# Plain float32 products for compressed keys, values and queries, compressed biases on TensorE, and a later layer norm, in a hybrid decoder block

## The chip, the core and the metric

The kernel runs on one core of one Trainium2 chip. The metric is the device time of one execution in microseconds (us). The engines of the core run side by side, each with its own in-order queue: PE (TensorE, matrix products; PEld is its loading of weights), DVE (VectorE), ACT (ScalarE), POOL (GpSimd) and SP, which here only issues transfers.

## The reference

One decoder layer for 256 positions and 1024 features, float32 throughout. Cut to what matters here:

```python
h = rms_norm(x, norm_mix_g)
u_conv, q, kc, vc, ks, vs, kw, vw, g_heads, g_conv, g_attn = split(h @ w_in)
# conv: gated, causal depthwise with 31 taps over 1024 channels, layer norm, silu, pointwise
v = a * sigmoid(gt); v = depthwise31(v) + dw_b
conv_out = silu(layer_norm(v, ln_g, ln_b)) @ pw_w
# compressed branch: 15 blocks of 32 keys, stride 16
k_cmp = silu((kc_blocks + pos) @ w1) @ w2          # the same for v_cmp
s_c = q @ k_cmp * scale + rel_bias[bucket(t - c_end)]
o_cmp = masked_softmax(s_c, t - c_end >= 0) @ v_cmp
# selected and window branches: for 256 positions both see every causal key,
# each with its own keys and values, both with rel_bias[bucket(t - k)]
o = g0 * o_cmp + g1 * o_slc + g2 * o_win
x = x + (sigmoid(g_conv) * conv_out + sigmoid(g_attn) * o) @ w_out
x = x + cross_attention(rms_norm(x), mem)
x = x + swiglu(rms_norm(x)); out = rms_norm(x)
```

There are 16 heads of 64 features in 4 key groups; kc, vc, ks, vs, kw and vw have 256 columns each, q has 1024. The bias depends only on the distance, through 32 buckets.

## The kernel before

Features lie on the 128 partitions, positions in the free dimension. The weights are streamed in chunks of 1024 x 256 (named k0 to k3, u0 to u7, kc, vc, q0 to q3, ks, kw, vs, vw, ga0 to ga3 and so on); a chunk comes in two halves of 512 KB, each a transfer on SP into one of three load tiles (tag "w", L138 and L139).

*Split products.* Almost every product is made from three matmuls in the format fp32r. `split` (L126) parts a half chunk into a rounded part `hi` (a copy on ACT, L129) and a rest `lo` (a subtraction, L131, on DVE; for a few early halves on POOL). The activations are parted in the same way (`hh`, `hl` for h). `product` (L146) then multiplies hi by hi, hi by lo and lo by hi. `gemm` (L151) does so for a whole chunk: 2 blocks of columns x 8 blocks of features x 3 = 48 matmuls into one PSUM bank, taken in turn from two (`bank`, L97, tag "mm"). The tags "s", "s0", "pt" and "o" hold six more banks for scores, transposes, the convolution's sums and outputs.

*The order.* The text of the kernel is the order in which instructions are offered; the framework's scheduler puts them into each engine's queue by a priority and by the times that it expects, so that work offered later (or with `tc.cur_priority` pushed back, L324) fills gaps. `tc.issue_after(x)` holds work behind x in that planning. Once built, each queue is fixed, and each engine goes through its own in order.

The stages around the change, in their order:

1. u0 to u7 give the gated convolution input `vt` (L284 to L288).
2. The 31 taps. Channels 0 and 1, and 4 and 5, are done by ACT and POOL (`taps_g`, L309): ACT multiplies into `vw` (L319, two buffers; every sixth tap POOL itself, L317), POOL adds into `yt` (L321). Channels 2 and 3 are done by DVE with sums in PSUM (`taps_v`, L304, tile `yp`), 6 and 7 by both, joined at L307. All of it is offered late, so it fills gaps for some 150 us.
3. The bias table: `relt` is loaded, one plain float32 matmul gives one row of 384 biases for each head (L336), and sixteen stores on SP (`table`, L343) spread it into a table `negb` in HBM, 16 x 128 x 256, put between the weight loads of kc to kw.
4. kc and vc (L360): the product, four copies into `kct` or `vct`, the addition of positions into `zin` (L372), 16 plain float32 matmuls with `w1t` into `z_ps` (L380), and the second small product.
5. q0 to q3 (L412): the product, then parted by ACT and DVE into `qt`. Then ks and kw (parted into `kdh` and `kdl`, L427), vs and vw, the head gates (L445), and ga0 to ga3 (L469).
6. Compressed scores (L480 to L507): 32 small matmuls `cs_ps`, joined into `nsc`, then for each pair of heads a load of the table (`nbc`, 256 KB) and two strided additions (L493), then minimum, exponential and sum.
7. `layer_norm_sums` and `layer_norm_scale` (L597, L618), offered before the pairs: POOL adds up `yt`, a matmul `mu` gives the mean, DVE subtracts, ACT squares, POOL adds, two small matmuls give `rl`, DVE multiplies.
8. Eight pairs of heads (`pair`, L517), each with a load `nb` of its rows of the table; between them the chunks gc0 to gc3 and v0 to v3 as filler. Then silu, pw, wo, cross-attention and the feed-forward part.

Long-lived tiles share numbered slots in SBUF (`long(name, slot)`, L82): `hf`, the float32 h, has slot 9 up to L275, then `w1t`, then `kdh`; `xr`, a second load of x for the residual (L689), has slot 14.

Of the kernel before, what the change touches and what calls it, by code (L numbers as in the profile page):

```python
# [58 lines left out]

@with_exitstack  # L60
def tile_hybrid_block(
# [10 lines left out]
    rel: bass.AP,  # L72
    out: bass.AP,
# [235 lines left out]
    def taps_g(j, begin):  # L309

        y = yt[:, j:j + 2]
        for t in range(begin, TAPS):
# [7 lines left out]
            if t > begin:  # L320
                nc.gpsimd.tensor_tensor(out=y, in0=y, in1=pr, op=ALU.add)  # L321

    here = tc.cur_priority
# [9 lines left out]
    relt = small("relt", [P, 512], tag="w", bufs=3)  # L333
    nc.sync.dma_start(relt, rel)
    rel_ps = aux("rel_ps", [P, 384], "s", 2)
    nc.tensor.matmul(rel_ps, lhsT=relt[:, 0:P], rhs=relt[:, P:512],  # L336
                     start=True, stop=True)
    rel_sb = small("rel_sb", [HEADS, 384], tag="pr", bufs=4)
    nc.scalar.activation(rel_sb, rel_ps[:HEADS], AF.Copy)
    negb = drp.tile([HEADS, P, S], F32, name="negb")  # L340
    row = rel_sb[:]

    def table(i):  # L343

        nc.sync.dma_start(negb[:, 8 * i:8 * i + 8], bass.AP(tensor=row.tensor, offset=row.offset + P - 1 - 8 * i,
                                                            ap=[list(row.ap[0]), [-1, 8], [1, S]]))
# [8 lines left out]
    w1t = long("w1t", 9, (P, 2, 16, HD))  # L355
# [3 lines left out]
    nc.vector.memset(zz, 0.0)  # L359
    for kv, name in enumerate(("kc", "vc")):  # L360
# [8 lines left out]
        zin = long(f"zin{kv}", (10, 14)[kv], (P, 16, GROUPS, 16))  # L369
        nc.vector.memset(zin[:, :, :, NCMP:], 0.0)  # L370
        view = kc[:]
# [40 lines left out]
    for j in range(4):  # L412
        ps = gemm(f"q{j}", h)
        for i in range(2):
            table(4 + 2 * j + i)
        q0, q1 = ([qt[j // 2][:, 4 * (j % 2) + 2 * b + k] for b in range(2)] for k in range(2))
        for b in range(2):
            nc.scalar.activation(q0[b][0:64], ps[0:64, b], AF.Copy, scale=-0.125)
            nc.scalar.activation(q1[b][64:128], ps[64:128, b], AF.Copy, scale=-0.125)
        for b in range(2):  # L420
            nc.vector.scalar_tensor_tensor(out=q0[b][64:128], in0=ps[0:64, b], scalar=-0.125, in1=f(q0[b][0:64]),
                                           op0=ALU.mult, op1=ALU.subtract)
# [4 lines left out]
    kdh, kdl = (long(n, i, (P, GROUPS, 2, S), F32R) for n, i in (("kdh", 9), ("kdl", 10)))  # L427
    for br, name in enumerate(("ks", "kw")):
        ps = gemm(name, h)
        for i in range(2):  # L430
            table(12 + 2 * br + i)
# [48 lines left out]
    nsc = small("nsc", [P, 2, HEADS, 16], tag="pr", bufs=4)  # L480
    for qb in range(2):
# [3 lines left out]
        nc.scalar.activation(nsc[:, qb], cs_ps[:, :, 0], AF.Copy)  # L485
        nc.vector.tensor_tensor(out=nsc[:, qb], in0=cs_ps[:, :, 1], in1=nsc[:, qb], op=ALU.add)
    for qb, n in ((1, NCMP), (0, 7)):
        nc.vector.memset(nsc[:, qb, :, n:], BIG)
    for hp in range(8):
        nb = bias_of(hp, "nbc")  # L490
        hs = slice(2 * hp, 2 * hp + 2)
        for qb, off, n in ((1, 31, NCMP), (0, 159, 7)):
            nc.vector.tensor_tensor(out=nsc[:, qb, hs, 0:n], in0=nsc[:, qb, hs, 0:n],  # L493
                                    in1=nb[:, :, off::16][:, :, 0:n], op=ALU.add)
# [22 lines left out]
    def pair(hp):  # L517
        heads = (2 * hp, 2 * hp + 1)
        g = heads[0] // 4
        nbp = bias_of(hp, "nb")  # L520
# [136 lines left out]
    yh, yl = longs(("yh", "yl"), (9, 10))  # L657
# [30 lines left out]
    xr = long("xr", 14)  # L688
    nc.sync.dma_start(xr, xt)  # L689
# [108 lines left out]
def _buckets():  # L798

    half = BUCKETS // 2  # L800
    ratio = MAX_DIST // half
    res = []
    for n in range(S):
        if n < half:
            res.append(n)
            continue
        b = half
        while b < BUCKETS - 1 and n ** half >= half ** half * ratio ** (b + 1 - half):
            b += 1
        res.append(b)  # L810
    return res


# [89 lines left out]
```

## Time and profile before

| | |
|---|---|
| median of 3 runs | 598.36 us (597.0 to 598.94) |
| the profiled execution, its own time | 597.25 us |
| its span, first to last instruction | 595.5 us |
| mean granted TensorE clock | 0.984 |
| instructions | 11133 |
| moved by transfers | 101.48 MB, mean 170 GB/s |

The page's part 1 gives each engine's busy time, its part 2 forty equal slices of the span (14.9 us each) with the busy share in tenths. Views of the trace name an instruction by line, engine, operation and tile (written <- read), with its shape and count; behind the bar stand busy time, mean duration in ns of one, and the idle time of the engine ahead of it with what ended that. A plain float32 matmul leaves two records in the trace, one in fp32r leaves one. Matmuls overlap: the distance between two starts, not the duration of one, is what a matmul costs in a row of them.

### The profile page before, as it was taken

Reading aid. Unit: us, or ns where it says so; the run is one execution under the profiler, and the core shown is the slowest. Engines: PE = TensorE matmul, PEld = TensorE weight load, DVE = VectorE, ACT = ScalarE, POOL = GpSimd, SP = SyncE. Lnnn points to the kernel's source line nnn. Section 1 sums busy time; section 2 is a strip of 40 time slices with the busy share of each in tenths; the row PEclk is TensorE's granted clock in tenths of the full one; section 3 lists DMA queues with packets and bytes.
Section 4 is the critical chain, followed back from the end, with each engine's and each line's share of the span. In section 5 each row is a group of like instructions: output and inputs, shape, how many; then the busy total and the mean of one; then the engine's idle time right before and its main releaser. Section 6 shows DMA issues by size and latency. Waiting matters only on the chain.

```text
span 595.5 us, 11133 instructions
## 1 busy us (share of the span) xinstructions
PE 561.8 (94%) x4248; PEld 531.5 (89%) x4248; DVE 447.5 (75%) x807; ACT 382.1 (64%) x712; POOL 177.8 (30%) x127
## 2 busy tenths in 40 slices
PE   8999895969899889999999999999999999999995
PEld 7889895969899889888999999998888888899995
DVE  5585798889999999977675957577877877854542
ACT  5557686377775789969844666467666566554440
POOL 0344997688799934000000300041000000000000
PEclk9999999898899999999999999999999999999998
DMA  8755568763577535321355554145556556566631
GB/s 291 244 181 176 197 179 194 200 222 105 147 232 236 194 114 187 123 85 68 126 180 188 180 166 153 66 153 182 204 176 210 179 177 210 177 176 184 191 89 70
DMA packets 34789, 101.48 MB, mean 170 GB/s; under 512 B 3632, under 2 KB 11184, under 8 KB 34480
## 3 DMA queue, kind: packets, MB, share of 16 engines
q1 hardware_dynamic: 33008, 98.67, 51.6%
q10 hardware_dynamic: 1728, 2.10, 1.3%
q8 instruction: 33, 0.54, 0.3%
q14 instruction: 20, 0.16, 0.1%
HBM read 96.56 MB, written 3.15 MB: 167 GB/s over the span
## 4 chain that ended last, share of the span: by engine, by line
PE 64%; DVE 15%; DMA 7%; issue 6%; ACT 5%; POOL 3%; DVEq 0%; SPq 0%; ACTq 0%; POOLq 0%
PE ps_f L745 14%; PE ps_f L747 7%; DVE yp L304 4%; PE fo L149 4%; PE fo L148 4%; PE fo L147 4%; DMA q<-in_wst_dram 3%; DMA k<-in_wst_dram 2%; PE ps_xq L148 1%; PE ps_pw L148 1%; PE ps_xo L148 1%; PE ps_v L149 1%; PE ps_xq L147 1%; PE ps_xq L149 1%; PE ps_xo L147 1%
## 5 line engine op out<-in xcount | busy, mean ns | idle before, releaser
L321 POOL TENSOR_TENSOR yt<-yt,vw 128x512 f32<-128x512 f32 x69 | 113.3, 1643 | 34.0 <-ACT vw L319 29.9
L319 ACT ACTIVATE vw<-vt,ppt 128x256 f32<-128x256 f32 x114 | 51.0, 499 | 23.6 <-POOL yt L321 23.2
L745 PE MATMUL ps_f<-g,f_1h 128*128 128x512 f32 x176 | 47.9, 391 | 0.0
L745 PE MATMUL ps_f<-g,f_0h 128*128 128x512 f32 x176 | 47.7, 394 | 0.0
L304 DVE SCALAR_TENSOR_TENSOR yp<-vt,ppt,yp 128x256 f32<-128x256 f32 x98 | 43.8, 479 | 0.7
L131 DVE TENSOR_TENSOR f_0l<-f,f_0h 128x1024 fp32r<-128x1024 f32 x22 | 27.5, 1249 | 21.9 <-ACT sl L752 21.0
L778 POOL COPY acc<-s 128x256 f32<-128x256 f32 x1 | 0.8, 815 | 134.2 <-ACT s L776 134.2
L745 PEld LDWEIGHTS ps_f<-g,f_1h 128*128 128x128 f32 x176 | 33.0, 188 | 7.5 <-DVE g L680 0.4
L745 PEld LDWEIGHTS ps_f<-g,f_0h 128*128 128x128 f32 x176 | 30.4, 190 | 4.1
L748 ACT ACTIVATE ab<-ps_f 128x256 f32<-128x256 f32 x44 | 16.4, 374 | 23.7 <-PE ps_f L747 23.7
L129 ACT ACTIVATE f_0h<-f 128x1024 fp32r<-128x1024 f32 x22 | 23.3, 1060 | 12.8 <-PE ps_f L745 9.7
L683 POOL COPY acc<-s_wo 128x256 f32<-128x256 f32 x1 | 0.9, 934 | 100.1 <-ACT s_wo L676 100.1
L747 PEld LDWEIGHTS ps_f<-g,f_0l 128*128 128x128 f32 x176 | 26.9, 189 | 3.3
L747 PE MATMUL ps_f<-g,f_1l 128*128 128x256 f32 x176 | 28.4, 283 | 0.0
L747 PE MATMUL ps_f<-g,f_0l 128*128 128x256 f32 x176 | 28.0, 282 | 0.0
L131 DVE TENSOR_TENSOR f_1l<-f,f_1h 128x1024 fp32r<-128x1024 f32 x22 | 26.9, 1221 | 0.7 <-ACT f_1h L129 0.7
L747 PEld LDWEIGHTS ps_f<-g,f_1l 128*128 128x128 f32 x176 | 24.3, 192 | 0.0
L129 ACT ACTIVATE f_1h<-f 128x1024 fp32r<-128x1024 f32 x22 | 23.1, 1049 | 1.2 <-DMA f<-in_wst_dram 1.1
L317 POOL TENSOR_SCALAR vw<-vt,ppt 128x256 f32<-128x256 f32 x24 | 21.5, 907 | 0.8
L147 PE MATMUL ps_u<-hh,u_0h 128*128 128x256 f32 x64 | 18.5, 289 | 2.1 <-DVE vt L288 2.1
L131 DVE TENSOR_TENSOR u_1l<-u,u_1h 128x1024 fp32r<-128x1024 f32 x8 | 14.1, 1765 | 7.3 <-ACT u_1h L129 7.3
L148 PE MATMUL ps_u<-hl,u_0h 128*128 128x256 f32 x64 | 18.2, 284 | 1.3 <-DVE hl L207 1.3
(547 smaller groups left out, 2287.7 us busy)
## 6 DMA issues: line engine op xcount, KB each, us to landing
f<-in_wst_dram SPq DMA_DIRECT2D x44, 512.0 KB, 3.8
fo<-in_wfo_dram SPq DMA_DIRECT2D x20, 512.0 KB, 3.8
u<-in_wst_dram SPq DMA_DIRECT2D x16, 512.0 KB, 4.3
q<-in_wst_dram SPq DMA_DIRECT2D x8, 512.0 KB, 6.3
ga<-in_wst_dram SPq DMA_DIRECT2D x8, 512.0 KB, 4.0
gc<-in_wst_dram SPq DMA_DIRECT2D x8, 512.0 KB, 3.7
v<-in_wst_dram SPq DMA_DIRECT2D x8, 512.0 KB, 3.7
pw<-in_wst_dram SPq DMA_DIRECT2D x8, 512.0 KB, 3.6
```

What stands on the lines that cost most here:

```text
L129: nc.scalar.activation(hi, w, AF.Copy)
L131: eng.tensor_tensor(out=lo, in0=w, in1=f(hi[:]), op=ALU.subtract)
L147: nc.tensor.matmul(o, lhsT=wh, rhs=xh, start=start, stop=False)
L148: nc.tensor.matmul(o, lhsT=wh, rhs=xl, start=False, stop=False)
L149: nc.tensor.matmul(o, lhsT=wl, rhs=xh, start=False, stop=stop)
L304: nc.vector.scalar_tensor_tensor(out=yt[:, k] if last else acc[:, i], in0=v, scalar=w, in1=acc[:, i], op0=ALU.mult, op1=ALU.add)
L317: nc.gpsimd.tensor_scalar(out=pr[:, i], in0=v, scalar1=w, scalar2=0.0, op0=ALU.mult, op1=ALU.add)
L319: nc.scalar.activation(pr[:, i], v, AF.Identity, scale=w, bias=col(PP_DB, j + i) if t == 0 else 0.0)
L321: nc.gpsimd.tensor_tensor(out=y, in0=y, in1=pr, op=ALU.add)
L745: nc.tensor.matmul(ps, lhsT=hs[kb // 4][0][:, kb % 4, cs], rhs=fg[:, :, kb], start=kb == 0, stop=False)
L747: nc.tensor.matmul(ps[:, 1], lhsT=hs[kb // 4][1][:, kb % 4, cs], rhs=fg[:, 0, kb], start=False, stop=kb == NB - 1)
L748: nc.scalar.activation(ab[:, b], ps[:, 0], AF.Copy)
```

## The change

- `bank` may take chunks' banks in turn from the two "mm" banks and the two "s" banks, from the taps up to the pairs.
- kc, vc and q0 to q3 are multiplied by a new function `whole`: no splitting; the load tile itself and `hf` are the operands of plain float32 matmuls, 16 for a chunk. `hf` therefore lives until q3, and several tiles change their slots (`w1t` 14, `kdh` 10, `kdl` 14, `xr` 9). kc and vc share one tile `kvt`, their position sums one tile `zins`.
- The compressed biases are made by TensorE: a new input `cb` (4 x 128 x 256; one-hot rows of buckets, with a mask row) is loaded, and for each half of the positions four small plain matmuls with columns of a longer `relt` give `cb_ps`, which ACT copies into `nsc`. The scores `cs_ps` are added to that in four DVE additions, and the eight `nbc` loads, the sixteen additions of L493 and two memsets go.
- The table in HBM goes as well. One store writes each head's row of 384 eight times (`line`); each pair reads its shifted rows from it in two transfers of 128 KB.
- `layer_norm_sums` is offered behind the third pair, `layer_norm_scale` behind the fourth. The load of `xr` is offered behind the last pair's scores.

```diff
     def bank(name):
+        four.append(0)
+        if "s" in four[0] and len(four) % 2:
+            return axp.tile([P, 2, S], F32, tag="s", name=name, bufs=2)
         return mmp.tile([P, 2, S], F32, tag="mm", name=name)
+    four = [""]
...
+    def whole(name, x):
+        ps = bank(f"ps_{name}")
+        for at in range(0, NB, 4):
+            w = small(f"{name}_{at}", [P, 4, 256], tag="w", bufs=3)
+            loads.append(nc.sync.dma_start(w, wst[CHUNK_AT[name]][:, at:at + 4]).ins)
+            for k in range(4):
+                kb = at + k
+                for b in range(2):
+                    cs = slice(b * P, b * P + P)
+                    nc.tensor.matmul(ps[:, b], lhsT=w[:, k, cs], rhs=x[:, kb], start=kb + b == 0, stop=kb == NB - 1 and b == 1)
+        return ps
...
+    four[0] = "s"
     here = tc.cur_priority
...
-    relt = small("relt", [P, 512], tag="w", bufs=3)
+    relt = small("relt", [P, RT_END], tag="w", bufs=3)
     nc.sync.dma_start(relt, rel)
+    cbt = small("cbt", [P, len(CGROUPS), S], tag="w", bufs=3)
+    nc.sync.dma_start(cbt, cb)
...
+    nsc = small("nsc", [P, 2, HEADS, 16], tag="pr", bufs=4)
+    cb_ps = aux("cb_ps", [P, 2, 16, HEADS], "s", 2)
+    for qb in range(2):
+        for i, ns in enumerate(CGROUPS):
+            n0, n1 = ns[0], ns[-1] + 1
+            nc.tensor.matmul(cb_ps[:, qb, n0:n1].rearrange("p n h -> p (n h)"), lhsT=cbt[:, i, qb * P:qb * P + P],
+                             rhs=relt[:, RT_CB + 16 * n0:RT_CB + 16 * n1], start=True, stop=True)
+    nc.scalar.activation(nsc, cb_ps.rearrange("p q n h -> p q h n"), AF.Copy)
...
-    negb = drp.tile([HEADS, P, S], F32, name="negb")
-    row = rel_sb[:]
-    def table(i):
-        nc.sync.dma_start(negb[:, 8 * i:8 * i + 8], bass.AP(tensor=row.tensor, offset=row.offset + P - 1 - 8 * i,
-                                                            ap=[list(row.ap[0]), [-1, 8], [1, S]]))
-    def bias_of(hp, name):
-        t = small(f"{name}{hp}", [P, 2, S], tag="nb", bufs=2)
-        nc.sync.dma_start(t, negb[2 * hp:2 * hp + 2].rearrange("h q k -> q h k"))
+    line = drp.tile([HEADS, 8, 384], F32, name="line")
+    nc.sync.dma_start(line, rel_sb.unsqueeze(1).to_broadcast([HEADS, 8, 384]))
+    row = line[:]
+    def bias_of(hp):
+        t = small(f"nb{hp}", [P, 2, S], tag="nb", bufs=2)
+        for k in range(2):
+            nc.sync.dma_start(t[:, k], bass.AP(tensor=row.tensor, offset=row.offset + 8 * 384 * (2 * hp + k) + P - 1,
+                                               ap=[[384 - 16, 8], [-1, 16], [1, S]]))
         return t
...
     for kv, name in enumerate(("kc", "vc")):
-        ps = gemm(name, h)
-        for i in range(2):
-            table(2 * kv + i)
-        kc = long(f"{name}t", 11 + 2 * kv, (P, GROUPS, S))
+        ps = whole(name, hf)
+        kc = kvt[:, kv]
...
     for j in range(4):
-        ps = gemm(f"q{j}", h)
-        for i in range(2):
-            table(4 + 2 * j + i)
+        ps = whole(f"q{j}", hf)
...
-        nc.scalar.activation(nsc[:, qb], cs_ps[:, :, 0], AF.Copy)
-        nc.vector.tensor_tensor(out=nsc[:, qb], in0=cs_ps[:, :, 1], in1=nsc[:, qb], op=ALU.add)
-    for qb, n in ((1, NCMP), (0, 7)):
-        nc.vector.memset(nsc[:, qb, :, n:], BIG)
-    for hp in range(8):
-        nb = bias_of(hp, "nbc")
-        hs = slice(2 * hp, 2 * hp + 2)
-        for qb, off, n in ((1, 31, NCMP), (0, 159, 7)):
-            nc.vector.tensor_tensor(out=nsc[:, qb, hs, 0:n], in0=nsc[:, qb, hs, 0:n],
-                                    in1=nb[:, :, off::16][:, :, 0:n], op=ALU.add)
+        for i in range(2):
+            nc.vector.tensor_tensor(out=nsc[:, qb], in0=cs_ps[:, :, i], in1=nsc[:, qb], op=ALU.add)
...
-    total = layer_norm_sums()
-    layer_norm_scale(total)
+    four[0] = ""
     for hp, names in enumerate(("gc0", "gc1", "gc2", "gc3", "v0", "v1", "", "v2 v3")):
         mark, exp = pair(hp)
...
-        if hp == -1:
+        if hp == 2:
             total = layer_norm_sums()
-        if hp == -1:
+        if hp == 3:
             layer_norm_scale(total)
...
-    xr = long("xr", 14)
-    nc.sync.dma_start(xr, xt)
+    xr = long("xr", 9)
+    with tc.issue_after(mark):
+        nc.sync.dma_start(xr, xt)
```

More of the change, by code (lines that the diff above doesn't have):

```diff
@@ L57, with _buckets, _groups @@
 CP_END = CP_HM + 8
+def _buckets():
+    half = BUCKETS // 2
+    ratio = MAX_DIST // half
+    res = []
+    for n in range(S):
+        if n < half:
+            res.append(n)
+            continue
+        b = half
+        while b < BUCKETS - 1 and n ** half >= half ** half * ratio ** (b + 1 - half):
+            b += 1
+        res.append(b)
+    return res
+def _groups():
+    far = [S - 1 - (16 * n + 31) for n in range(16)]
+    rows = [(_buckets()[d] + 1 if d >= 0 else 0) + 1 for d in far]
+    groups, n = [], 0
+    while n < 16:
+        m = n
+        while m < 16 and sum(rows[n:m + 1]) <= P:
+            m += 1
+        groups.append(list(range(n, m)))
+        n = m
+    return rows, groups
+CROWS, CGROUPS = _groups()
+RT_CB = 512
+RT_END = RT_CB + 16 * HEADS
 @with_exitstack
@@ L359, in tile_hybrid_block @@
     nc.vector.memset(zz, 0.0)
+    kvt = long("kvt", 11, (P, 2, GROUPS, S))
+    zins = long("zins", 13, (P, 2, 16, GROUPS, 16))
     for kv, name in enumerate(("kc", "vc")):
[L361 to L364 removed]
+        ps = whole(name, hf)
+        kc = kvt[:, kv]
         nc.scalar.activation(kc[0:64, 0::2, :], ps[0:64], AF.Copy)
@@ L368, in tile_hybrid_block @@
         nc.vector.tensor_copy(kc[64:128, 1::2, 0:S - 1], ps[64:128, :, 1:S])
-        zin = long(f"zin{kv}", (10, 14)[kv], (P, 16, GROUPS, 16))
+        zin = zins[:, kv]
         nc.vector.memset(zin[:, :, :, NCMP:], 0.0)
-        view = kc[:]
+        view = kc
         nc.vector.tensor_tensor(
@@ L424, in tile_hybrid_block @@
                                            op0=ALU.mult, op1=ALU.subtract)
-    kdh, kdl = (long(n, i, (P, GROUPS, 2, S), F32R) for n, i in (("kdh", 9), ("kdl", 10)))
+    kdh, kdl = (long(n, i, (P, GROUPS, 2, S), F32R) for n, i in (("kdh", 10), ("kdl", 14)))
     for br, name in enumerate(("ks", "kw")):
         ps = gemm(name, h)
-        for i in range(2):
-            table(12 + 2 * br + i)
         for lo, g in ((0, 0), (64, 1)):
@@ L795, in tile_hybrid_block @@
         nc.sync.dma_start(out[:, ks], x3[:, ks])
[L798 to L811, printed above, removed]
 _OUTS = [((P, NB, S), "float32")]
```

26 lines of the change are left out of this document (20 added, 6 removed).

## The prediction

> **What bounds the kernel now.** I read the page's shares and slices first, then the busy time of four stretches, then the gaps inside the slow ones.
>
> ```profile
> PE 561.8 (94%) x4248; PEld 531.5 (89%) x4248; DVE 447.5 (75%) x807; ACT 382.1 (64%) x712; POOL 177.8 (30%) x127
> PE   8999895969899889999999999999999999999995
> DVE  5585798889999999977675957577877877854542
> POOL 0344997688799934000000300041000000000000
> ```
>
> Averages hide two regimes. From slice 17 on PE stands at 9 and nothing else sets the time. Between slices 5 and 15 PE drops to 5, 6 and 8 while DVE and POOL stand at 8 and 9. The stretches below are cut at the end of the last u chunk (84.4), of q3 (139.2), of ga3 (202.3) and of the last pair (298).
>
> ```profile
> 84.40:139.20 54.80, 43.89 (x361) 42.15 (x360) 47.61 (x66) 36.85 (x75) 41.61 (x30) 0.94 0.71 191
> 139.20:202.30 63.10, 57.29 (x446) 56.35 (x445) 62.60 (x102) 44.26 (x80) 56.64 (x39) 0.95 0.61 190
> 202.30:298.00 95.70, 92.74 (x751) 83.56 (x750) 80.47 (x266) 81.83 (x210) 18.32 (x13) 1.00 0.37 122
> 298.00:590.00 292.00, 289.97 (x2094) 273.95 (x2092) 198.06 (x292) 164.67 (x264) 16.75 (x18) 1.00 0.51 165
> ```
>
> Columns are length, then busy time (count) of PE, PEld, DVE, ACT, POOL, then granted clock. Stage A (kc, vc, q0 to q3) loses 10.9 us of PE, stage B (ks to ga3) 5.8 us while DVE is busy 62.6 of 63.1, stage C (pairs) 3.0. After 298 PE is full, and the change edits nothing there. So only A, B and C can move. What the loss in A looks like:
>
> ```profile
> 98.31 0.28 PE L149 MATMUL ps_vc<-hh,vc_1l 128*128 128x256 f32 x1
> 103.06 0.55 PE L147 MATMUL ps_q<-hh,q_0h 128*128 128x256 f32 x1 [4.47 <-ACT q_0h L129]
> 103.41 0.41 PE L148 MATMUL ps_q<-hl,q_0h 128*128 128x256 f32 x1
> 103.62 0.41 PE L149 MATMUL ps_q<-hh,q_0l 128*128 128x256 f32 x1
> 95.64 6.60 SPq L345 DMA_DIRECT2D negb<-rel_sb  x5
> 102.35 1.28 SPq L139 DMA_DIRECT2D q<-in_wst_dram  x1
> ```
>
> q's first half is late, PE stands for over 4 us, and then its matmuls follow each other at 0.21 us where 0.12 is normal: the granted clock is down, which the 0.94 of stage A contains. Meanwhile the load queue issues table stores; a q load gets out only at 102.35.
>
> **The change part by part.**
>
> *Plain products.* Six chunks lose 2 splits each on ACT and on DVE, and 48 matmuls become 16 plain float32 ones.
>
> ```profile
> 257.02 0.28 PE L149 MATMUL ps_v<-v_1h,meml 128*128 128x256 f32 x1
> 257.14 0.28 PE L147 MATMUL ps_v<-v_0h,memh 128*128 128x256 f32 x1
> 257.26 0.59 PE L570 MATMUL o<-pct,vals 128*128 128x256 f32 x2
> 257.79 0.44 PE L576 MATMUL o<-ptt_b,vals 128*64 128x128 f32 x4
> L570 PE MATMUL o<-pct,vals 128*128 128x256 f32 x16 | 4.7, 378 | 0.0
> 109.97 2.08 PE L380 MATMUL z_ps<-zin,w1t 128*64 128x64 f32 x32
> ```
>
> A split matmul follows the last at 0.12 us, so a chunk is 48 x 0.12 = 5.7 us. A plain one of the same shape leaves two records (L570: 16 for 8 pairs). The two end 0.59 after the first begins and one lasts 0.378, so they start 0.21 apart; the next tile starts 0.53 after the first. A plain matmul thus costs between 2 x 0.21 = 0.43 and 0.53. In a run of equal ones I take 0.43: 16 x 0.43 = 6.9 us a chunk, **+1.1 to 1.2 each, +7 for six** (+16 at 0.53). What is removed on DVE:
>
> ```profile
> L131 DVE TENSOR_TENSOR q_0l<-q,q_0h 128x1024 fp32r<-128x1024 f32 x4 | 7.6, 1912 | 1.5 <-ACT q_0h L129 1.5
> L131 DVE TENSOR_TENSOR q_1l<-q,q_1h 128x1024 fp32r<-128x1024 f32 x4 | 5.1, 1278 | 4.6 <-ACT q_1h L129 4.6
> L131 DVE TENSOR_TENSOR vc_1l<-vc,vc_1h 128x1024 fp32r<-128x1024 f32 x1 | 1.9, 1917 | 0.0
> L304 DVE SCALAR_TENSOR_TENSOR yp<-vt,ppt,yp 128x256 f32<-128x256 f32 x89 | 39.5, 479 | 0.5
> L493 DVE TENSOR_TENSOR nsc<-nsc,nbc 128x14 f32<-128x14 f32 (+1 forms) x16 | 5.0, 364 | 0.0
> L131 DVE TENSOR_TENSOR v_1l<-v,v_1h 128x1024 fp32r<-128x1024 f32 x4 | 4.9, 1217 | 0.0
> ```
>
> 7.6 + 5.1 for q and 4 x 1.9 for kc and vc: 20 us of DVE; with L493's 5.0, 25 us in A and B. In the order of the changed kernel all DVE taps (L304) then stand ahead of the first ks split, so DVE does them in A, in the place of the splits, and in B it has the 17 splits (at 1.9, 32 us) and little else. DVE stops being the bound of B.
>
> *The weight buffers.* A plain chunk multiplies straight from the load tile, of which there are three, so a tile is held until 8 matmuls (3.4 us) have run. Loading and using must fit in 3 x 3.4 = 10.3 us, so a load may take 6.9.
>
> ```profile
> q<-in_wst_dram SPq DMA_DIRECT2D x8, 512.0 KB, 6.3
> negb<-rel_sb SPq DMA_DIRECT2D x16, 128.0 KB, 5.3
> nbc<-negb SPq DMA_DIRECT2D x8, 256.0 KB, 3.8
> kc<-in_wst_dram SPq DMA_DIRECT2D x2, 512.0 KB, 4.3
> ```
>
> 4.3 fits well, 6.3 just. Two hiccups remain. relt and the new cbt (512 KB) sit in the same three tiles until the new cb_ps matmuls behind u7, so kc's second half is issued only then: 4.3 us against 3.4 us of work ahead of it, with vc's load beside it, 1 to 3 us, taken 2. And four bias loads stand on SP ahead of q0, behind the store of `line`; that store (192 KB, bounded by nbc's 3.8 and twice negb's 5.3) waits for ACT, the bias loads wait for the store, every weight load behind them waits too: 0 to 6 us at q0, taken 2.
>
> *Tables.* 16 stores of negb and 8 loads of nbc (2 MB each way) go, with their places on SP; one store and 4 early loads come, and 16 half-size loads for the pairs instead of 8. The pairs' extra issues are hidden, since SP there has gaps of microseconds between weight loads. The compressed bias becomes 8 small plain matmuls, 16 records like those of z_ps (32 in 2.08): about 1 us on PE, unhidden.
>
> ```profile
> L402 PE MATMUL vc_ps<-ppt,zz 128*128 128x64 f32 x4 | 0.7, 287 | 0.5 <-DVE zz L388 0.5
> ```
>
> Stage A after: 6 x 6.9 + two z_ps of 2.1 + 1 for the bias + 1 for vc_ps (0.7) and its like + 2 + 2 = **51.6 against 54.8, -3**. Floor without hiccups 47.5 (-7); at 0.53 a matmul 61 (+6).
>
> *Four banks* cost nothing: PE may run two chunks further ahead of ACT's evictions. Without them an eviction that is late (next paragraph) would stop PE one chunk later.
>
> *POOL and ACT.* ACT multiplies taps (vw, two buffers), POOL adds them.
>
> ```profile
> L319 ACT ACTIVATE vw<-vt,ppt 128x256 f32<-128x256 f32 x94 | 42.0, 499 | 19.3 <-POOL yt L321 19.1
> L321 POOL TENSOR_TENSOR yt<-yt,vw 128x512 f32<-128x512 f32 x69 | 113.3, 1643 | 34.0 <-ACT vw L319 29.9
> 84.40:209.70 125.30, 88.25 (x54) 0.95 0.65 189
> 84.40:209.70 125.30, 16.15 (x18) 0.95 0.65 189
> 190.35 11.11 POOL L321 TENSOR_TENSOR yt<-yt,vw 128x512 f32<-128x512 f32 x6
> 208.33 1.31 POOL L321 TENSOR_TENSOR yt<-yt,vw 128x512 f32<-128x512 f32 x1
> L129 ACT ACTIVATE q_1h<-q 128x1024 fp32r<-128x1024 f32 x4 | 4.2, 1056 | 10.4 <-DMA q<-in_wst_dram 10.4
> ```
>
> ACT no longer stands 10.4 us before q's loads, so POOL starves less. But POOL's own work is fixed: the two stretch rows are POOL's adds of L321 (54 from 84.4 on) and its own multiplies of L317 (18, 16 us). At 1.31 an add (DVE quiet) it ends at 84.4 + 71 + 16 = 172; at 11.11/6 = 1.85 at 200; at 1.45 for the 30 in A and 1.75 for the 24 in B, with 2 idle, at 188. The changed ACT order puts the last vw just ahead of ga3's splits, and the DVE order puts the sum of POOL's part (L307) ahead of ga3's last split. So B can't end before POOL: 188 + 0.7 + a split of 1.5 + three quarters of a chunk, 4.3 = **194.5**. By PE alone, B is 8 chunks x 5.7 + the gates' 24 x 0.12 = 48.7 us, plus 2 at ks, where load, ACT and DVE start again from an empty ring: 84.4 + 51.6 + 51 = 187. Where ACT waits for POOL, evictions and ks's splits behind it are late too. I take **193, between, nearer POOL: -9.3 for A and B together**.
>
> *Stage C.* cs_ps moves behind ga3, and the layer norm behind the third and fourth pair.
>
> ```profile
> L484 PE MATMUL cs_ps<-kcp,qt 128*128 128x32 f32 x32 | 4.5, 262 | 1.2 <-DVE qt L421 1.0 <-ACT qt L419 0.2
> PE mu L604 <- POOL ysum L215: 1.6, 1, 1.6
> ```
>
> cs_ps brings 4 us of PE into C, of which the 3.0 lost there can hold some; mu's wait of 1.6 goes if POOL is long done by the third pair, yet the norm's DVE and ACT work stays between pairs. Bounds -3 to +8, taken **+2**. xr's megabyte is needed only behind 298; moving it to the slot of hf is free under 100 us of pairs.
>
> Sum against the profiled execution (597.25, of which 1.75 lies outside its span of 595.5): 597.25 - 9.3 + 2 = **590**; against the median of the runs shown, 598.36, that is 8.4 less.
>
> A rule that speaks against the change: the Trainium skill, "TensorE: Matmul & The Clock Gate", section "HAM oscillation — how this bites in real kernels", says a PE gap over about 3.4 us drops the clock to half, and load-bound loops pay it again for each tile. The trace agrees at 98.31 to 103.06. By it a late q0 (the 0 to 6 above) would cost twice; it is the third rival's trigger.
>
> **The rivals.**
>
> *PE bound, POOL keeps up.* POOL adds run at 1.31 with the splits gone from A; B ends at 187, C costs nothing: 597.25 - 15.3 = 582, 579 without hiccups. For it: 1.31 beside a quiet DVE. Against: 17 splits remain in B.
>
> *Layer norm between pairs returns the gain.* mu, the norm's two small products and its DVE work stand in in-order queues between pairs; three waits like mu's 1.6 to 3 plus cs_ps's 4.5 make +8 to +9 in C: 597. For it: ACT is busy 82 and DVE 80 of 95.7 already. Against: the same work stood there before, one pair earlier.
>
> *Plain chunks starve* (slower). Place: the three-tile ring in A. If loads among the bias loads take more than 6.9 us, each half leaves a gap, the clock falls as at 103.41, and a plain chunk takes 0.21/0.12 times 6.9 = 12: three chunks +15, stalls +4, so A ends 16 us later than before, and B then saves 10: 597.25 + 16 - 10 + 2 = 605. It decides from loads of 7 us on. For it: q's 6.3 already. Against: the 16 slow table stores that stood beside q are gone.
>
> **How the numbers follow.** Forecast 590 (own range 584 to 596): 0.47. PE bound, 582: 0.24. Norm returns it, 597: 0.15. Starving, 605: 0.14. A run of this kernel can tell 0.3%, 1.8 us. Faster than 596.6: 0.46 + 0.24 + 0.06 = 0.76; within: 0.01 + 0.08 = 0.09; slower: 0.14 + 0.01 = 0.15. The range 578 to 600 leaves out the starving case and the far end of the second.
>
> **What would show it.** The new lines for plain products must show records 0.21 apart and no idle over 3 us in front of them; the end of q3 at 133 to 138; the last POOL add between 180 and 190 and ga3's end 3 to 6 us behind it; DVE in B well under 62 of 63. If the last add lies at 175 and ga3 ends near 187, the first rival holds. If PEclk falls for most of A, the third. If the stretch from ga3's end to the last pair grows beyond 100 us, the second. The forecast is wrong altogether if stage 298 to the end changes length.

## The result and the profile after

The changed kernel takes 590.84 us (590.2 to 592.1 in four runs) against 598.53 for the kernel before on the same chip: a ratio of 0.987, 95% interval 0.984 to 0.990. The forecast was 590. The profiled execution has a span of 588.5 us, 7.0 less than before. One execution among all those below took 1088 us, nearly twice as long as the others of its kernel (the new tables alone), and is left out; it was the profiled one, so no trace of that kernel is read.

The first lines are from parts 1 and 2 of the page of the changed kernel; below them stands the view by stretches, cut at the same events as before: the end of the last u chunk (85.6), of q3 (134.8), of ga3 (192.8), and the last pair.

```profile
PE 566.1 (96%) x4168; PEld 531.6 (90%) x4168; DVE 418.8 (71%) x779; ACT 371.6 (63%) x699; POOL 164.8 (28%) x127
PE   8989899996999999999999999999999999999995
DVE  5585799997566788878576867587787787764542
POOL 0343999999789000210000400050000000000000
PEclk9999899997999999999999999999999999999997
```

```profile
85.60:134.80 49.20, 48.53 (x280) 42.42 (x278) 47.10 (x102) 31.76 (x75) 46.21 (x41) 1.00 0.48 155
134.80:192.80 58.00, 52.57 (x412) 51.15 (x411) 37.88 (x34) 40.42 (x68) 50.90 (x35) 0.94 0.65 205
192.80:290.40 97.60, 96.10 (x785) 87.54 (x785) 75.31 (x263) 80.45 (x207) 5.50 (x4) 1.00 0.37 122
290.40:582.40 292.00, 289.94 (x2094) 273.69 (x2092) 198.19 (x290) 165.22 (x265) 16.66 (x17) 1.00 0.51 165
```

Stage A (kc to q3) went from 54.8 to 49.2 us, and PE is busy 48.5 of it at full clock. DVE is still busy 47 of 49, now with taps instead of splits. Stage B (ks to ga3) went from 63.1 to 58.0; DVE's busy time there fell from 62.6 to 37.9, so it no longer bounds the stage, yet PE still loses 5.4 us and the mean clock is 0.94. The 6 in slice 10 of the PE row, the only one below 8 ahead of the last slice, shows where: from 132 to 147 us, at the start of B.

Stage A in the timeline of PE (start, length, instruction, count, idle before):

```profile
85.63 1.92 PE L404 MATMUL cb_ps<-relt,cbt 128*128 128x48 f32 x16
87.39 3.65 PE L231 MATMUL ps_kc<-hf,kc 128*128 128x256 f32 x16
91.70 3.72 PE L231 MATMUL ps_kc<-hf,kc 128*128 128x256 f32 x16 [0.67 <-DMA kc<-in_wst_dram]
95.26 7.07 PE L231 MATMUL ps_vc<-hf,vc 128*128 128x256 f32 x32
102.17 2.10 PE L231 MATMUL ps_q<-hf,q 128*128 128x256 f32 x9
```

vc's 16 plain products leave 32 records and take 6.9 us up to the next chunk's start (102.17 - 95.26), 0.43 each. The only wait for a load is 0.67 us at kc's second half; q0 follows vc without one. The 4.5 us stop of before and the half clock behind it are gone.

The start of B: first the timeline of ACT, then the waits of PE (waited for, sum, times, longest).

```profile
133.76 1.04 ACT L173 ACTIVATE ks_0h<-ks 128x1024 fp32r<-128x1024 f32 x1
135.22 0.91 ACT L376 ACTIVATE vw<-vt,ppt 128x256 f32<-128x256 f32 x2 [0.42 <-POOL yt L378]
136.57 0.91 ACT L376 ACTIVATE vw<-vt,ppt 128x256 f32<-128x256 f32 x2 [0.44 <-POOL yt L378]
138.80 0.91 ACT L376 ACTIVATE vw<-vt,ppt 128x256 f32<-128x256 f32 x2 [1.32 <-POOL yt L378]
139.61 1.04 ACT L173 ACTIVATE ks_1h<-ks 128x1024 fp32r<-128x1024 f32 x1
```

```profile
PE ps_ks L193 <- DVE ks_0l L175: 2.3, 1, 2.3
PE ps_ks L191 <- ACT ks_1h L173: 1.3, 1, 1.3
PE ps_ks L193 <- DVE ks_1l L175: 1.1, 1, 1.1
```

Between the two splits of ks three pairs of taps stand in ACT's queue, and each waits for POOL to free one of the two `vw` buffers. So ks_1h comes almost 6 us behind ks_0h, and PE waits 1.3 us for it and 1.1 us for the rest `lo` made from it. The longest wait of the three, 2.3 us for ks_0l, has another place, the queue of DVE:

```profile
131.34 3.12 DVE L361 SCALAR_TENSOR_TENSOR yp<-vt,ppt,yp 128x256 f32<-128x256 f32 x6
136.23 1.39 DVE L175 TENSOR_TENSOR ks_0l<-ks,ks_0h 128x1024 fp32r<-128x1024 f32 x1
```

Six of DVE's taps and, behind them, four operations on parts of q stand ahead of ks_0l, so it begins 1.4 us after ks_0h is done (134.80). With these waits, and with a lower clock behind them (last section), ks, which needs 5.7 us of PE, takes 13.

The end of B, from the timelines of POOL, DVE and PE:

```profile
184.99 1.30 POOL L378 TENSOR_TENSOR yt<-yt,vw 128x512 f32<-128x512 f32 x1
```

```profile
186.32 0.69 DVE L364 TENSOR_TENSOR yt<-yp,yt 128x512 f32<-128x512 f32 x1 [3.83 <-POOL yt L378]
186.93 1.70 DVE L175 TENSOR_TENSOR ga_1l<-ga,ga_1h 128x1024 fp32r<-128x1024 f32 x1
```

```profile
188.32 0.28 PE L191 MATMUL ps_ga<-hh,ga_1h 128*128 128x256 f32 x1
188.44 0.28 PE L192 MATMUL ps_ga<-hl,ga_1h 128*128 128x256 f32 x1
188.68 0.39 PE L193 MATMUL ps_ga<-hh,ga_1l 128*128 128x256 f32 x1
```

This is the chain that the prediction worked out: POOL's last add ends at 186.3, DVE has stood 3.83 us for it, the split of ga3's second half follows and ends at 188.6, and PE's first use of it starts at 188.68. But PE gets there itself at 188.56: the distance from 188.44 is 0.24 instead of 0.12. PE's own pace and POOL's chain arrive within 0.12 us of each other.

### The profile page after: what moved, and what is told of

The parts are those of the page before. It is cut to its first block, busy times and chain, and to the rows that moved or that the text cites. A ratio compares the mean times of both kernels' runs of the same rounds, so it can differ in the third digit from the quotient of the medians.

```text
span 588.5 us, 10882 instructions
## 1 busy us (share of the span) xinstructions
PE 566.1 (96%) x4168; PEld 531.6 (90%) x4168; DVE 418.8 (71%) x779; ACT 371.6 (63%) x699; POOL 164.8 (28%) x127
## 4 chain that ended last, share of the span: by engine, by line
PE 61%; POOL 13%; ACT 10%; DMA 7%; DVE 6%; issue 2%; SPq 0%; ACTq 0%; DVEq 0%; POOLq 0%
PE ps_f L799 14%; POOL yt L378 11%; PE ps_f L801 7%; PE fo L193 4%; PE fo L192 4%; PE fo L191 4%; ACT vw L376 2%; DMA ga<-in_wst_dram 2%; DMA k<-in_wst_dram 2%; DMA u<-in_wst_dram 2%; PE ps_xo L192 1%; PE ps_gc L193 1%; PE ps_gc L191 1%; PE ps_gc L192 1%; PE ps_pw L191 1%
## 5 line engine op out<-in xcount | busy, mean ns | idle before, releaser
L378 POOL TENSOR_TENSOR yt<-yt,vw 128x512 f32<-128x512 f32 x69 | 106.6, 1546 | 23.9 <-ACT vw L376 19.5
L361 DVE SCALAR_TENSOR_TENSOR yp<-vt,ppt,yp 128x256 f32<-128x256 f32 x98 | 42.2, 481 | 0.9
L173 ACT ACTIVATE f_0h<-f 128x1024 fp32r<-128x1024 f32 x22 | 23.3, 1060 | 13.2 <-PE ps_f L799 10.2
L231 PE MATMUL ps_q<-hf,q 128*128 128x256 f32 x128 | 28.8, 382 | 0.0
L231 PEld LDWEIGHTS ps_q<-hf,q 128*128 128x128 f32 x128 | 24.0, 190 | 3.2
L669 POOL TENSOR_TENSOR ssum<-ssum,sq 128x512 f32<-128x512 f32 x3 | 4.8, 1588 | 55.5 <-ACT sq L668 55.3
```

The costliest lines, as they stand in the source:

```text
L173: nc.scalar.activation(hi, w, AF.Copy)
L231: nc.tensor.matmul(ps[:, b], lhsT=w[:, k, cs], rhs=x[:, kb], start=kb + b == 0, stop=kb == NB - 1 and b == 1)
L361: nc.vector.scalar_tensor_tensor(out=yt[:, k] if last else acc[:, i], in0=v, scalar=w, in1=acc[:, i], op0=ALU.mult, op1=ALU.add)
```

## The experiments

Each kernel below is the changed one with one edit, unless it says otherwise. Stages are compared by the starts of last matmuls in PE's timelines: from the last u to ga3's last (A and B, 107.2 us in the changed kernel, 117.9 before), in it from q3's last to ks's last (13.3; 11.4), and from ga3's last to the first of wo (C, 114.9; 113.2). The last u itself comes at 83.3 to 87.2 in the profiled executions that are read here, though nothing ahead of it differs, so one span is good to about 2 us, and the medians decide. Each ratio is against the kernel before on the same chip; its medians there are 597.7 to 598.9, so medians of two experiments compare to about 1 us.

**Split products again**

```diff
-        ps = whole(name, hf)
+        ps = gemm(name, h)
...
-        ps = whole(f"q{j}", hf)
+        ps = gemm(f"q{j}", h)
```

> The changed kernel with kc, vc and q0 to q3 multiplied as split products again (ACT and DVE part the weights, 48 fp32r matmuls a chunk); tables, norm and banks as changed. Theory (the gain comes from DVE and ACT work taken out of the kc-to-q stage, so that taps are done earlier; PE pays about 7 us for it): the 20 us of DVE splits return, ga3 ends 5 to 8 us later than the changed kernel's 192.7, time 595 to 599. Rival (the gain comes from the sixteen table stores and eight bias loads taken off the load queue; plain products only cost): PE needs 7 us less, ga3 ends at 186 to 189, time 584 to 588.

Measured: 592.4 us (591.8 to 595.4), ratio 0.9915 (0.989 to 0.994), between the two expectations. A and B got shorter, 104.5 us: ks took 7.7. C grew to 119.8. The timeline of POOL in that kernel, and that of DVE:

```profile
203.06 1.29 POOL L378 TENSOR_TENSOR yt<-yt,vw 128x512 f32<-128x512 f32 x1
```

```profile
204.38 0.69 DVE L364 TENSOR_TENSOR yt<-yp,yt 128x512 f32<-128x512 f32 x1 [3.75 <-POOL yt L378]
```

POOL ends 18 us later than in the changed kernel, and DVE waits for it in C. PE's longest wait in C is for ACT:

```profile
PE cs_ps L546 <- ACT sga L530: 2.0, 1, 2.0
```

`cs_ps` takes its bank over from a ga chunk, and ACT empties that bank (into `sga`) only behind splits and taps in its queue. The groups of POOL between 85 and 198 us say why (shapes, count, busy, mean ns of one, idle before), first of the changed kernel, then of this one:

```profile
L378 POOL TENSOR_TENSOR yt<-yt,vw 128x512 f32<-128x512 f32 x53 | 80.7, 1524 | 8.4 <-ACT vw L376 5.0
L374 POOL TENSOR_SCALAR vw<-vt,ppt 128x256 f32<-128x256 f32 x18 | 11.2, 635 | 0.2
```

```profile
L378 POOL TENSOR_TENSOR yt<-yt,vw 128x512 f32<-128x512 f32 x50 | 85.8, 1716 | 10.2 <-ACT vw L376 7.3
L374 POOL TENSOR_SCALAR vw<-vt,ppt 128x256 f32<-128x256 f32 x19 | 17.9, 951 | 0.6
```

With the twelve splits back on DVE, the same add takes 0.19 us longer and the same multiply 0.32: some 50 adds and 19 multiplies make 15.6 of the 18 us. By the medians the plain products thus gain 1.6 us net, though single runs of the two kernels overlap (590.2 to 592.1 and 591.8 to 595.4). The gain isn't PE's, which they cost 1.2 us a chunk; what they change is that GpSimd gets its taps done earlier.

**Split products, and GpSimd relieved** (the run before, with `SHARE = 31`, so that VectorE does the last ten taps of channels 6 and 7)

> Split products for kc, vc and q (as in the earlier run, 592.4) and the last ten taps of channels 6 and 7 on VectorE, so that GpSimd is done early. It tells why the stage behind ga3 was 5 us longer with split products. Theory: GpSimd, busy to 204 to 207 there, was late for the norm; with its end at about 180 the stretch from ga3 to the first wo goes back from 119.7 to 115 to 116.5 us, and the time to 588 to 590, that is, plain products would be worth nothing by themselves. Rival: the stretch stays at 118 to 121 us (it is VectorE or the place of cs_ps, not GpSimd), 592 to 595.

Measured: 591.6 us (591.1 to 592.0), ratio 0.988 (0.986 to 0.990), between theory and rival in time; the stretch behind ga3, 119.1 us, is the rival's. GpSimd's adds were done at 182, and then, in its timeline:

```profile
221.53 1.29 POOL L656 TENSOR_TENSOR ysum<-ysum,yt 128x512 f32<-128x512 f32 x1 [32.06 <-DVE yt L361]
```

Now VectorE, with splits and taps, is 32 us late with its part and does it among the pairs. So GpSimd's late end was one form of it: whichever of the two has the taps, the work that the splits push out of A and B comes up in C. With this `SHARE` and plain products the time is 591.6 us as well (the kernel with `SHARE = 31` alone, further below): A and B take 4.0 us less here and C 4.2 more. At this `SHARE` the plain products are worth nothing in time.

**Two banks**

```diff
-    four[0] = "s"
```

> The changed kernel with the two 'mm' banks alone for chunks. Theory (evictions by ACT come late behind POOL by a few us, which two banks cover): 0 to +2 us, time 590 to 593. Rival (ACT's evictions wait for POOL so long that PE needs four banks): PE idle ahead of q1, q2 or q3 of 3 us or more each, time 596 or more.

Measured: 594.9 us (592.8 to 596.9), ratio 0.994 (0.992 to 0.996). The four banks are worth 4.1 us. A and B take 112.5 us. One of PE's waits in that kernel:

```profile
PE cs_ps L545 <- DVE qt L485: 2.0, 1, 2.0
```

The scheduler puts `cs_ps` back into A and B there: 10 of its 32 matmuls ahead of q3, the others up to 158.2 us (4 us of PE work that the changed kernel does in C). Ahead of the tenth PE waits 2.0 us for DVE's part of q. C, without that work, is 114.3, hardly shorter; its mean granted clock is 0.97 instead of 1.00. No wait of PE for an eviction stands among this kernel's waits, so neither expectation had the mechanism: the two banks cost time through the order that the scheduler chose with them.

**The tables of before, with the plain products.** The stores of `negb`, the loads of `nbc` and the DVE additions return, `cb_ps` goes.

```diff
-    line = drp.tile([HEADS, 8, 384], F32, name="line")
-    nc.sync.dma_start(line, rel_sb.unsqueeze(1).to_broadcast([HEADS, 8, 384]))
+    negb = drp.tile([HEADS, P, S], F32, name="negb")
...
         ps = whole(name, hf)
+        for i in range(2):
+            table(2 * kv + i)
```

> The changed kernel with the bias tables of before (16 stores of negb, eight loads of nbc, adds on DVE; no products for the compressed bias), so that the plain products run beside the slow table traffic. Theory: the tables' stores stand ahead of a weight load of q, PE stands for 3 to 6 us there as before, two or three of the halves behind it are late, and DVE gets 5 us of adds back; 595 to 600. Rival, the forecast's starving case: with only three load tiles each plain chunk waits for its load and runs at half rate, stage A ends 10 us or more later, 601 to 608. Rival, the tables were hidden: 590 to 592, and the whole gain is the plain products, banks and order.

Measured: 612.8 us (609.8 to 613.9), ratio 1.023 (1.019 to 1.026), slower than the kernel before and than every expectation. A and B take 114.9 us, C 131.0. The timeline of SP in that kernel (length of an issue row: from its first to its last issue), then PE's waits:

```profile
79.14 0.33 SPq L226 DMA_DIRECT2D vc<-in_wst_dram  x1
82.30 14.43 SPq L404 DMA_DIRECT2D negb<-rel_sb  x12
96.84 1.32 SPq L226 DMA_DIRECT2D vc<-in_wst_dram  x1
```

```profile
PE s L589 <- DVE mins L595: 9.3, 1, 9.3
PE ps_vc L231 <- DMA vc<-in_wst_dram: 7.8, 1, 7.8
```

Twelve stores, 1.2 us an issue, stand ahead of vc's second half, and PE waits 7.8 us for it. In C the `nbc` loads stand behind seven weight loads in the same queue, and the pairs wait 9.3 us for DVE, which waits for `nbc`. Two thirds of the loss against the changed kernel lie in C. PE did starve in A, but not as the starving rival had it: vc's loads took 5.6 us and q's 3.4 (median from issue to landing), well under its threshold of 7. What was late was the issue. The scheduler placed the stores in another way than in the kernel before, so this run prices that placement, and not the tables as such.

**The new tables alone**: split products, two banks and the norm first, so that of the change only the tables, the biases by TensorE and the moved tiles stay.

> Of the change only the new tables: split products for kc, vc and q, two banks, norm ahead of the first pair; the compressed biases by TensorE, one store and direct bias loads stay. If the parts measured alone add up (plain products worth 1.6 us, four banks 4.1, the norm's place costing 2.7), it is 590.8 + 1.6 + 4.1 - 2.7 = 593.8, a range of 592 to 596: the tables would be worth about 4.7 us by themselves, and most of the change. Rival: the tables are worth little without the plain products, because VectorE, with its splits, is the bound of ks to ga3 as before: 597 to 599.

Measured: 594.7 us (593.7 to 595.1), ratio 0.993 (0.991 to 0.996), inside the range that the sum of the parts gave. The new tables, with the biases by TensorE and the moved tiles, are worth 3 to 4 us by the medians.

**The norm ahead of the first pair**

```diff
+    total = layer_norm_sums()
+    layer_norm_scale(total)
     four[0] = ""
     for hp, names in enumerate(("gc0", "gc1", "gc2", "gc3", "v0", "v1", "", "v2 v3")):
...
-        if hp == 2:
+        if hp == -1:
             total = layer_norm_sums()
-        if hp == 3:
+        if hp == -1:
             layer_norm_scale(total)
```

> The changed kernel with the layer norm ahead of the first pair again. Theory (its place is worth little, POOL's part ends at 191 in any case): PE waits 1 to 3 us more around the first pairs, time 591 to 594. Rival (the norm among the pairs is what costs the 2 to 3 us that the stage of the pairs lost): time 586 to 589.

Measured: 588.1 us (586.3 to 588.9), ratio 0.984 (0.982 to 0.986); its slowest run is below the fastest of the changed kernel. C takes 112.6 us instead of 114.9. Of the parts measured alone the later norm is the one that costs time, some 2.7 us. `mu` had waited 1.6 us for POOL before; here POOL is done ahead of it, and PE's waits show none in C. In the changed kernel it has three there, 1.5 us together, one of them (0.6 us) for `z`, which is made from the norm's result.

**GpSimd freed of channels 6 and 7**

```diff
-SHARE = 21
+SHARE = 31
```

> The changed kernel with SHARE 31: the ten taps of channels 6 and 7 that ACT and POOL did go to DVE (20 more operations of 0.48 us, 9.6 us on DVE; 10 adds of about 1.6 us and 4 multiplies of 0.9 off POOL, 16 multiplies of 0.5 off ACT). Theory (POOL's adds pace the stage up to ga3): the last add lies near 167 instead of 186.3, the 3.8 us for which DVE waits for POOL ahead of ga3's last split go, ga3 ends at 187 to 189, time 585 to 588. Rival 1 (the loads or PE pace that stage, POOL only looks late): no change, 590 to 592. Rival 2 (DVE is the bound there): ga3 ends 4 to 9 us later, 594 to 599.

Measured: 591.6 us (589.6 to 592.3), ratio 0.9885 (0.986 to 0.991). POOL's adds end at 165.6, yet ga3 ends 109.8 us behind the last u, 2.5 later than in the changed kernel: ks took 14.9, with this wait of PE:

```profile
PE ps_ks L193 <- DVE ks_0l L175: 3.7, 1, 3.7
```

The added taps stand on DVE ahead of ks's split. So an early end of POOL alone doesn't bring an early end of B. What it would be worth with ks as it was stays open, since the edit itself made ks 1.6 us longer.

**The split of ks ahead of the last taps on ACT**

```diff
-    taps_g(4, 0)
+    taps_g(4, 0, 19)
     taps_v(2, TAPS)
-    taps_g(6, SHARE)
-    taps_v(6, SHARE)
...
         ps = gemm(name, h)
+        if br == 0:
+            here = tc.cur_priority
+            tc.cur_priority = here + 1500
+            with tc.issue_after(splits[-1]):
+                taps_g(4, 19, start=0)
+                taps_g(6, SHARE)
+                taps_v(6, SHARE)
+            tc.cur_priority = here
```

(`splits` holds the ACT halves of all splits so far; `taps_g` gets an end. The edit does more than its expectation says: the taps of channels 6 and 7 are offered later too. On DVE that changed little: ahead of ks_0l stand six taps and four operations on q, as in the changed kernel.)

> The second split of ks is put ahead of the last taps of channels 4 and 5 in ACT's order; nothing else. Theory: in the changed kernel ks took 13.0 us of PE (134.86 to 147.91) instead of 5.7, because ks_1h stood on ACT behind three pairs of vw that waited for POOL (1.32, 0.44 and 0.42 us) and began only at 139.61. With the split ahead, ks_1h begins at 135 to 137.5, ks ends at 143 to 145.5, ga3 at 188 to 190.5, and the time falls by 2 to 4 us from 590.8, to 587 to 589. Rival 1, the load ring: ks_1 lands late anyway (its tile is held by q3's plain matmuls), ks_1h begins after 138.5, time 590 to 592. Rival 2: ks ends early, but POOL, which gets its taps later, is late for an eviction or the norm, and the time stays at 590 to 592 although ga3 ends before 190.5.

Measured: 591.3 us (590.6 to 594.6), ratio 0.9885 (0.985 to 0.992). The second rival held in its time and its cause, though ga3 ended at 192.5, not before 190.5. ks took 9.6 us instead of 13.3. PE's waits for ks_1h and ks_1l fell from 2.4 to 0.5 us, the wait for ks_0l is as long as before, and this time the matmuls behind it kept the full clock:

```profile
138.85 0.39 PE L194 MATMUL ps_ks<-hh,ks_0l 128*128 128x256 f32 x1 [2.32 <-DVE ks_0l L175]
```

But A and B together took only 0.9 us less (106.4): PE now waits 0.9 us for each part of vs's second half. C took 119.2. The timelines of POOL and DVE, then PE's waits in the start of C:

```profile
192.14 2.25 POOL L380 TENSOR_TENSOR yt<-yt,vw 128x512 f32<-128x512 f32 x1
```

```profile
194.42 0.69 DVE L365 TENSOR_TENSOR yt<-yp,yt 128x512 f32<-128x512 f32 x1 [1.16 <-POOL yt L380]
```

```profile
PE s L589 <- DVE nsc L556: 1.5, 1, 1.5
```

POOL gets its taps later and ends at 194.4 instead of 186.3. The sum on DVE waits for it, two splits and `nsc` stand behind that sum, and PE waits for `nsc`: the prediction's chain, 8 us on. The wait is 1.5 us, and from 195 to 212 us the mean granted clock is 0.80.

**Both: the early split, and the norm first**

> The early split of ks together with the layer norm ahead of the first pair. Theory (the two are in different stages, so they add): 588.1 less the 2 to 4 us of the early split, 584 to 586.5. Rival: the norm ahead of the pairs needs POOL's last tap, which the early split makes later, so the two do not add: 587 to 590.

Measured: 593.4 us (590.8 to 595.2), ratio 0.991 (0.987 to 0.994), beyond the rival's range. A and B took 102.9 us, the shortest of all, ks 7.8. Then:

```profile
PE mu L666 <- POOL ysum L273: 5.1, 1, 5.1
```

POOL's last sum ended at 197.3, and with the norm first PE itself stands for it. C grew to 120.1.

**Less for GpSimd, on top of both: five more taps of channels 6 and 7 on DVE** (`SHARE = 26`)

> As the run before with the early split of ks and the layer norm first (593.4), but channels 6 and 7 give five more taps to VectorE and so five fewer to ACT and GpSimd. Theory: GpSimd's end is the floor that all faster stages run into. There ga3 ended 102.9 us behind the last u chunk (107.2 in the changed kernel), and mu then stood 5.24 us for ysum, because GpSimd's last sum ended at 197.3. Five adds at 1.6 us and one of its multiplies less, GpSimd ends 8 to 10 us earlier, mu's wait is under 1 us, ga3 to the first wo 112 to 114 us instead of 120.1, and the time 582 to 586. Rival: VectorE's ten added taps (5 us) or ACT make something else late and the time stays at 588 to 593.

Measured: 587.7 us (587.3 to 588.3), ratio 0.982 (0.980 to 0.984). POOL's last sum ends at 189.3, mu's wait is gone and C is 112.6, as the theory had it. But ks took 13.2 again, with PE's wait of 3.1 us for ks_0l, because DVE's added taps stand ahead of it:

```profile
138.53 1.01 DVE L362 SCALAR_TENSOR_TENSOR yp<-vt,ppt,yp 128x256 f32<-128x256 f32 x2
139.46 1.22 DVE L175 TENSOR_TENSOR ks_0l<-ks,ks_0h 128x1024 fp32r<-128x1024 f32 x1
```

So the time missed the theory's 582 to 586 by what A and B kept (106.1 us instead of 102.9), and lies just under the rival's 588 to 593.

**No multiplies on GpSimd, on top of both** (`MIX = 99`)

> The same early split and norm first, but GpSimd multiplies no taps at all (ACT does all of them), the adds as in the changed kernel. Theory: GpSimd loses its multiplies (0.93 us each, 16 to 18 us from the last u chunk on), ends before 190, mu's wait goes and the time is 582 to 586. Rival: ACT, in whose order the added taps (0.5 us each, 8 to 10 us) stand ahead of splits and evictions, is late for PE in the stages to ga3; the stretch from the last u to ga3 grows from 102.9 to 106 or more, and the time is 586 to 592.

Measured: 590.0 us (589.6 to 593.3), ratio 0.986 (0.983 to 0.989). A and B 104.2 us, but POOL's last sum still ends at 196.2 and mu waits 3.7. The waits of POOL in that kernel:

```profile
POOL yt L380 <- ACT vw L378: 36.3, 18, 13.9
```

With both edits alone it had been 22.0 us. ACT, now with all multiplies, hands POOL its taps later, and that takes up what POOL saves.

**The taps of DVE behind ks too** (as the run with `SHARE = 26`; the taps 16 to 25 of DVE's part are offered behind the second `lo` of ks)

```diff
+    acc6 = taps_v(6, SHARE, stop=16)
...
+            with tc.issue_after(lows[-1]):
+                taps_v(6, SHARE, 16, acc6)
```

> As the run with the early split of ks, the norm first and five more VectorE taps for channels 6 and 7 (587.7), but the taps 16 to 25 of VectorE are put behind ks's second split on VectorE too. There ks still took 13.2 us from q3's end to its own end, with 3.1 us of PE waiting for ks_0l, because VectorE had taps ahead of the splits. Theory: with both splits early on both engines ks takes 7.5 to 9.5 us, the stretch from the last u to ga3 goes from 106.1 to 101.5 to 104, GpSimd still ends before 190, ga3 to the first wo stays at 112.6 to 114, and the time is 582.5 to 586. Rival: what ks gains comes back as at the first early split (a wait at vs, or VectorE late in the first pair), 586.5 to 590.

Measured: 588.4 us (586.5 to 589.2), ratio 0.982 (0.979 to 0.985). ks took 8.2 us, POOL ended at 181, C was 112.6, and A and B were still 106.3. PE's timeline shows where ks's gain went:

```profile
145.32 0.39 PE L195 MATMUL ps_kw<-hh,kw_0l 128*128 128x256 f32 x1 [2.03 <-DVE kw_0l L175]
161.33 0.39 PE L194 MATMUL ps_vw<-vw_1l,hh 128*128 128x256 f32 x1 [1.89 <-DVE vw_1l L175]
```

The taps put behind ks stand between the next splits on DVE, and kw and vw wait for those. The rival held in kind, with the waits at kw and vw.

No version got A, B and C short at once. Those with the norm first and POOL early enough, the plain edit of the norm among them, take 587.7 to 588.4 us and can't be told apart; the smallest edit that beats both kernels is the norm ahead of the pairs.

## Why the prediction was right, step by step

*Plain products.* Right. 0.43 us each, 6.9 a chunk, as taken. Of the two hiccups (2 us each) kc's was 0.67 and q0's nil, `cb_ps` took 1.8 instead of 1. A came out at 49.2 instead of 51.6, inside the bounds given. The step didn't say what they are worth in time: 1.6 us by the medians as the kernel stands, nothing with `SHARE = 31`.

*Tables.* Right in direction: the stop at q0 and its half clock went. The step had the tables as a part of A's sum only; measured alone they bring 3 to 4 us.

*Four banks cost nothing.* True and mis-sized: the step gave them no gain, and they bring 4.1 us. It gave a late eviction as what would stop PE without them; the run with two banks shows no such wait. It missed that the banks decide where the scheduler puts `cs_ps`.

*DVE stops being the bound of B.* Right: 37.9 of 58.0 us busy.

*POOL sets the end of B.* The chain was right to the instruction: last add forecast at 188, measured 186.3, and ga3 ending 6.5 us behind it, as the sum had it. The time of the last add is partly luck, for its terms were off by some 5 us each and cancel: in the groups of POOL above the adds took 80.7 us (forecast 85.5), the multiplies 11.2 (16), and POOL stood idle 8.6 (2). And the step took PE alone to be done at 187, with 2 us lost at ks; PE lost 7.5 us there and ended at the same moment as POOL. The prediction had itself put DVE's taps ahead of ks's first split, without a price for the wait. POOL's chain holds PE up by 0.12 us. So the forecast of 193 (192.7 measured) rests on two floors of equal height, one seen and one seen at a quarter of its size; that they met there is luck. The run that ended POOL at 165.6 gained nothing, which the POOL step alone can't explain (though ks was also longer there). The run that shortened ks by 3.7 us gained nothing either, which the ks stop alone can't explain: there POOL, later by 8 us, took it back in C, through the chain that the prediction had put in B.

*C, +2.* Right in sum (114.9 against 113.2, +1.7), with other parts: `cs_ps`'s 4 us fit into waits that went, and the later norm costs 2.3 us of C. The second rival, the norm giving back the gain, was right in kind and too large: 2.7 us in the medians instead of 7.

*The rivals.* POOL keeping up (582) fell at its own condition, adds of 1.31 us (they took 1.52 in the mean behind the last u), and at ks; by its own terms its 579 without hiccups should read 578. Starving (605) didn't happen, and in the run with the old tables it was the order in SP's queue, not the length of a load, that made PE starve in A.

The sum by the profiled spans: A and B -10.6, C +1.7, the rest +0.7, and the last u 1.2 later in this execution, together -7.0.

## What to carry to other kernels

When a stage ends with several engines, work out each one's end separately; where two lie within a us or two, removing one wait gains less than that wait, as the runs with `SHARE = 31`, with ks's split first, with both edits and with DVE's taps behind ks showed. Work that fills gaps in in-order queues (taps on ACT and DVE) is free only as long as nothing that PE waits for is queued behind it, so look at the first split of a new stage. And before a load is called slow, look at when it was issued.

## What the runs showed of the hardware

The clock fell after shorter stops than I had expected: in the changed kernel PE stood 2.3 us ahead of 137.67 and, after a short run, matmuls came 0.21 us apart from 138.8 on, until 145.3. ks took 7.5 us longer than its 5.7. Counted from start to start, the three stops make 5.5 us of that, and the half rate of 16 matmuls, with the slower steps around the stops, the other 2.0. The Trainium skill, "TensorE: Matmul & The Clock Gate", section "HAM oscillation — how this bites in real kernels", puts the gap that drops the clock at over about 3.4 us; here it fell after one of 2.3, and the measurement decides. But the length of one stop isn't all: in the run with ks's split first, a stop of the same 2.32 us (ahead of 138.85) left the clock at 1.00. What else decides, no run here shows; so some 2 of the 3.7 us that that run gained at ks may be the clock and not the split.

POOL's pace depends on which work DVE has, not on how much. The groups of POOL's adds in the changed kernel, first from 115.2 to 123.2 us, where DVE was busy but for 0.6 of 8 us, mostly with taps whose sums lie in PSUM, then from 139 to 186, where it had splits:

```profile
L378 POOL TENSOR_TENSOR yt<-yt,vw 128x512 f32<-128x512 f32 x6 | 7.6, 1271 | 0.5
```

```profile
L378 POOL TENSOR_TENSOR yt<-yt,vw 128x512 f32<-128x512 f32 x20 | 34.4, 1720 | 5.2 <-ACT vw L376 4.1
```

An add takes 1.27 us beside taps and 1.72 in the mean beside splits. A tap reads one operand from SBUF (`vt`) and one from PSUM, a split reads both from SBUF (the load tile and `hi`). The Trainium skill, "GPSIMD Engine Reference", section "1. Specifications", says that GpSimd shares its SBUF interfaces with VectorE and contends with VectorE instructions that have two SBUF inputs; these rows agree. Other work with both operands in SBUF does the same in stage A. Here are POOL and then DVE, with the addition of positions:

```profile
98.47 5.31 POOL L378 TENSOR_TENSOR yt<-yt,vw 128x512 f32<-128x512 f32 x3 [0.39 <-ACT vw L376]
```

```profile
100.02 2.67 DVE L439 TENSOR_TENSOR zins<-kvt,ppt 128x960 f32<-128x960 f32 x1
```

Of these three adds two took 1.3 us, and the third, from 101.17 on beside `zins`, 2.60. The forecast had seen 1.31 and 1.85 as DVE being quiet or busy. No run varied the operands of DVE's work alone.
